# Moving the padding between SBUF tiles in a Trainium2 transformer-block kernel

## The chip, the cores and the metric

The kernel runs on one core of a Trainium2 chip. The metric is the device time of one execution, in microseconds; the median of three runs is quoted. TensorE (PE) multiplies matrices: it loads a stationary operand of 128 columns (PEld, LDWEIGHTS) and streams a moving operand of up to 512 columns past it into PSUM. VectorE (DVE) and ScalarE (ACT) do elementwise work, and DMA brings the weights from HBM into SBUF, the on-chip memory from which PE reads both operands.

## What is computed

One layer of a diffusion transformer block over 256 latent tokens and 256 context tokens, width 2048, all in float32:

```python
sh_a, sc_a, g_a, sh_m, sc_m, g_m = ada_modulation(c, w_ada, b_ada)      # 2048 x 12288
h  = modulate(rms_norm(x, norm_attn_w), sh_a, sc_a)                     # and hc for ctx
q, k, v, u = split_projection(h @ w_in)                                 # 2048 x 2560
attn = latent_window_attention(rope(q), rope(k), v, kc, vc, sink)
pool = multiscale_pool(u, pool_w, pool_scale)
x  = x + g_a * (concat([attn, pool]) @ w_out)                           # 2048 x 2048
hm = modulate(rms_norm(x, norm_mlp_w), sh_m, sc_m)
x  = x + g_m * (square(relu(hm @ w_up)) @ w_down)                       # 2048 x 8192 x 2048
return rms_norm(x, final_norm_w)
```

## The kernel before, in words

Every large product is made of three passes. Both operands are split into a high and a low part of type float32r: `hi = round(a)` on ACT (L99) and `lo = a - hi` on DVE (L100) for weights, and likewise for the activations. A product of a (stationary) and b (moving) is then `a.hi*b.hi + a.hi*b.lo + a.lo*b.hi`, all three added up in one PSUM bank. The helper `mm3` issues them as lines 290, 291 and 292, in this order.

Weights come through one stream. A load on SP's queue brings 1 MB (four slices of 128 rows by 512 columns) into one of five `raw` tiles; each half of it is split into a `hi` and a `lo` tile of 4096 bytes per partition, of which there are six each. All loads are in one fixed order, worked out beforehand, in which the loads for the modulation vectors (`ada`) lie between those of the projections.

The stages, and which operand is stationary in each:

- the input projection: for q and u (`ps_qu`) and for k (`ps_k`) the weight is stationary and the modulated tokens `hhi`, `hlo` move, 256 columns for q and u, 512 for k; for v (`ps_v`) the tokens are stationary. The first weight tile has its own order of passes, line 497;
- attention and pooling, with the pooling products `ps_pool`;
- the output projection (`ps_w`): the mixed tokens `mx` are stationary, the weights move, 512 columns;
- the first three groups of the up projection (`first_up_groups`, lines 290 to 292 with `ps_up`): the weight is stationary and the tokens `mx` move, 256 columns;
- the other thirteen up groups (`up_group`, line 920): for each quarter of the contraction first 16 products with the weight's `hi` part stationary and both parts of `mx` moving at once, 512 columns, then 16 with the `lo` part stationary and the high part of `mx` moving, 256 columns;
- the down projection (`down_group`, `ps_d`): the squared activations `ahi`, `alo` are stationary, the weights move, 512 columns. Up and down groups alternate: two up groups, then 192 down products in a row.

Tiles lie in SBUF in pools; within a pool the tags follow each other in the order in which they are first asked for, each tag with all its buffers. `gap` (L50) asks for a tile that nothing uses, and so moves what comes after it by some bytes. All tiles of the products hold a multiple of 512 bytes per partition, and so do the steps between the slices that are used as operands, so that the addresses of a tag's tiles agree modulo 512.

Lines that the change touches: L97 puts 320 bytes between the `hi` and the `lo` tiles; L448 puts 320 bytes between `hhi` and `hlo` in each of the two pools `hpa` and `hpb`; L593 puts 192 bytes ahead of the `mx` tiles in `mixa`; L598 closes `hpa` with 320 bytes; L891 puts 64 bytes between `ahi` and `alo`.

Of the kernel before, what the change touches and what calls it, by code (L numbers as in the profile page):

```python
# [9 lines left out]
F32R = mybir.dt.float32r  # L10
# [5 lines left out]
P = 128  # L16
D = 2048
KC = 16
T = 256
# [30 lines left out]
def gap(pool, n, name="gap"):  # L50

    pool.tile([P, n // 4], F32, tag=name, name=name, bufs=1)


class WeightStream:
# [28 lines left out]
    def split_to(self, n):  # L88
        nc = self.nc
        while self.n_half < min(n, len(self.halves)) and not self.hold:  # L90
            i, h = self.halves[self.n_half]
            if i >= self.n_load:
                break
            raw = self.raw[i][:, 2 * h : 2 * h + 2, :]
            hi = self.pool.tile([P, 2, 512], F32R, tag="hi", name="hi", bufs=N_HALF)
            if not self.n_half:
                gap(self.pool, 320)  # L97
            lo = self.pool.tile([P, 2, 512], F32R, tag="lo", name="lo", bufs=N_HALF)
            up = nc.scalar.copy(hi, raw)  # L99
            low = nc.vector.tensor_tensor(lo, raw, hi.bitcast(F32), ALU.subtract)  # L100
            self.last = (up.ins, low.ins)
            self.split[i, h] = (hi, lo)
            self.n_half += 1
# [23 lines left out]
def kernel(  # L127
# [223 lines left out]
    hpa = hpa_es.enter_context(tc.tile_pool(name="hpa", bufs=1, side="right", reuse_waits="tile"))  # L351
# [48 lines left out]
    def normalize(i):  # L400

        ss4 = stp.tile([P, 4], F32, tag="ss4", name="ss4", bufs=2)
        ss = stp.tile([P, 1], F32, tag="ss", name="ss", bufs=2)
        for q in range(4):
            junk = stp.tile([P, 512], F32, tag="junk", name="junk", bufs=2)
            xq = xh[i][:, 512 * q : 512 * q + 512]
            if q % 2:
                nc.scalar.activation(junk, xq, AF.Square, accum_out=ss4[:, q : q + 1])
            else:
                nc.vector.scalar_tensor_tensor(junk, xq, 1.0, xq, ALU.mult, ALU.mult, accum_out=ss4[:, q : q + 1])  # L410
        nc.vector.tensor_reduce(ss, ss4, axis=AX.X, op=ALU.add)
        r = rstd(stp, ss, 1)
        nc.vector.tensor_scalar(xh[i], xh[i], r, None, ALU.mult)
        for g in range(4):
            tp = bank("tp")
            for j in range(4):
                k = 4 * g + j
                nc.tensor.transpose(tp[:, P * j : P * j + P], xh[i][:, P * k : P * k + P], ident)
            nc.scalar.copy(xT[g][:, :, P * i : P * i + P], tp.rearrange("p (j t) -> p j t", j=4))
# [22 lines left out]
    def modulated(c_, streams=(0, 1)):  # L442

        pool = hpb if c_ in (2, 3, 6, 7) else hpa
        if 0 in streams:
            hhi = pool.tile([P, 2, 512], F32R, tag="hhi", name="hhi", bufs=2)
            if c_ in (0, 2):
                gap(pool, 320, "gaph")  # L448
            hlo = pool.tile([P, 2, 512], F32R, tag="hlo", name="hlo", bufs=2)
            hparts[c_] = hhi, hlo  # L450
        hhi, hlo = hparts[c_]
        for j in range(2):
            k = 2 * c_ + j
            xk = xT[k // 4][:, k % 4, :]
            for s in streams:
                v = xk[:, T * s : T * s + T]
                nc.vector.tensor_scalar(v, v, am_a[:, k, s : s + 1], sm_a[:, k, s : s + 1], ALU.mult, ALU.add)
            ts_ = slice(T * streams[0], T * streams[-1] + T)
            up = nc.scalar.copy(hhi[:, j, ts_], xk[:, ts_])
            low = nc.vector.tensor_tensor(hlo[:, j, ts_], xk[:, ts_], hhi[:, j, ts_].bitcast(F32), ALU.subtract)  # L460
            hs[k] = lambda s, j=j: (hhi[:, j, s], hlo[:, j, s])
        return up.ins, low.ins
# [87 lines left out]
    def run_in(op):  # L550
        if op[0] == "ada":
            c_, kg = op[1:]
            if kg == 0:
                adas[c_] = ada_attn(c_)
            adas[c_][kg]()
        elif op[0] == "mod":
            adas[op[1]][4]()
            modulated(op[1])
        elif op[0] == "kv":
            project_kv(*op[1:])  # L560
        elif op[0] == "qu":
            project_qu(*op[1:])
        elif op[0] == "mean":
            pool_mean(op[1])
        elif op[0] == "mixb":
            open_mixb()
        elif op[0] == "pool":
            in_w["pool"] = S.next("w")
        elif op[0] == "poolp":
            pool_project(op[1])  # L570
        elif op[0] == "pools":
            pool_split(op[1])
        else:
            run_late(1)

    mixa = hpb = None

    cast, sub = modulated(0, (0,))
    S.hold = False
    with tc.issue_after(sub):  # L580
# [4 lines left out]
    for op in in_ops:  # L585
        if op[0] == "ctx":
            with tc.issue_after(first_split[0]), tc.issue_after(first_split[1]):
                normalize(2)
                normalize(3)
            modulated(0, (1,))  # L590
            xn_es.close()
            mixa = ctx.enter_context(tc.tile_pool(name="mixa", bufs=1, side="left", reuse_waits="tile"))
            gap(mixa, 192)  # L593
            hpb = hpb_es.enter_context(tc.tile_pool(name="hpb", bufs=1, side="left", reuse_waits="tile"))
            gap(hpb, 192)
        else:
            run_in(op)
    gap(hpa, 320)  # L598
    st_es.close()
    hpa_es.close()  # L600

# [222 lines left out]
    mp = ctx.enter_context(tc.tile_pool(name="mp", bufs=1, side="right", reuse_waits="tile"))  # L824
# [63 lines left out]

    def activation(pss):
        ahi = mp.tile([P, 4, T], F32R, tag="ahi", name="ahi", bufs=3)  # L890
        gap(mp, 64)  # L891
        alo = mp.tile([P, 4, T], F32R, tag="alo", name="alo", bufs=3)
        for m in range(4):
            t = mp.tile([P, T], F32, tag="act", name="act", bufs=2)
            if pss[m].shape[1] == T:
                nc.scalar.activation(t, pss[m], AF.Relu)
                nc.vector.tensor_tensor(t, t, t, ALU.mult)
            else:
                nc.scalar.copy(t, pss[m][:, T : 2 * T])
                nc.vector.tensor_tensor(t, pss[m][:, 0:T], t, ALU.add)  # L900
                nc.vector.scalar_tensor_tensor(t, t, 0.0, t, ALU.max, ALU.mult)
            nc.scalar.copy(ahi[:, m, :], t)
            nc.vector.tensor_tensor(alo[:, m, :], t, ahi[:, m, :].bitcast(F32), ALU.subtract)
        return ahi, alo

    def up_group():

        pss = [bank("ps_up") for _ in range(4)]
        for kg in range(4):
            w = S.next("w")
            for part in range(2):
                for m in range(4):
                    for j in range(4):
                        k = 4 * kg + j
                        wk = w(j, slice(P * m, P * m + P))[part]
                        ps, h = (pss[m][:, 0:T], hm[k][0]) if part else (pss[m], hm[k][2])
                        nc.tensor.matmul(ps, wk, h, start=part == k == 0, stop=part == 1 and k == KC - 1, skip_group_check=True)  # L920
        return activation(pss)

    def first_up_groups():

        banks = [bank("ps_up") for _ in range(6)]
        sums = [[banks[2 * f + m // 2][:, T * (m % 2) : T * (m % 2) + T] for m in range(4)] for f in range(3)]
        acts = []  # L930
        modulate_m(0)
        for kg in range(4):
            for f in range(3):
                w = S.next("w")
                if kg == f == 0:
                    with tc.issue_after(rb_ready.ins):
                        run_late(LATE_NORM)
                for m in range(4):
                    for j in range(4):
                        k = 4 * kg + j  # L940
                        mm3(sums[f][m], w(j, slice(P * m, P * m + P)), hm[k], k == 0 and m % 2 == 0, k == KC - 1)
                with tc.issue_after(rb_ready.ins):
                    run_late(LATE_UP[3 * kg + f])
                    if kg == 2 and f == 1:
                        run_late(1)
                if kg < 3 and f == 1:
                    modulate_m(kg + 1)
                if kg == 3:
                    acts.append(activation(sums[f]))
        return acts  # L950
# [152 lines left out]
```

## Time and profile before

| what | value |
|---|---|
| median of 3 runs | 1156.07 us (1155.22 to 1157.96) |
| the profiled execution, its own time | 1154.18 us |
| its span, first to last instruction | 1152.4 us |
| mean granted TensorE clock in it | 0.99 |
| PE busy | 1109.2 us, 96% of the span |
| DVE busy | 801.9 us, 70% |
| ACT busy | 504.9 us, 44% |
| HBM read | 283.50 MB |

The profiled execution lies 1.9 us below the median of the runs. A matmul's duration in the trace is longer than the distance in time from its start to the next one's, because matmuls overlap in the array's pipeline. So a busy share of 100% on PE says only that one matmul follows another; how fast they follow is seen from starts, or from durations of the same shape that are compared with each other.

### The profile page before, as it was taken

What the parts mean: (1) busy time and instruction counts of PE and PEld (TensorE: products, weight loads), DVE (VectorE), ACT (ScalarE), POOL (GpSimd) and SP (SyncE); (2) the same over time, 40 slices, a digit from 0 to 9 for tenths busy, and PEclk for the clock granted to TensorE, in tenths of its full rate; (3) what the DMA queues carried; (4) which work ended last, traced back from release to release, by engine and by line L of the source; (5) the groups of instructions that cost most, each with busy time, mean ns of one, the idle gap of its engine ahead of it and who ended that gap; (6) DMA issues with size and microseconds to landing.
All of it is one profiled execution on the core that took longest, in us unless ns stands there. A gap on an engine that the chain in (4) does not pass through costs nothing.

```text
span 1152.4 us, 16086 instructions
## 1 busy us (share of the span) xinstructions
PE 1109.2 (96%) x6332; PEld 903.4 (78%) x6332; DVE 801.9 (70%) x1286; ACT 504.9 (44%) x762; POOL 35.5 (3%) x53
## 2 busy tenths in 40 slices
PE   4999999979999989999999999999999999999996
PEld 3767778746578869988888888888888888888885
DVE  5655557988787888796775774784664665587576
ACT  4623233377634443365433444433444443443452
POOL 1000001610000000000000000000000000000000
PEclk9999999999999989999999999999999999999998
DMA  9999897667897999977775775676556556556532
GB/s 341 358 342 345 274 332 265 212 237 272 278 380 266 311 324 343 354 257 248 272 247 184 255 268 197 239 260 205 186 189 200 192 183 184 192 188 203 183 110 74
DMA packets 174012, 286.66 MB, mean 249 GB/s; under 512 B 5608, under 2 KB 72352, under 8 KB 172784
## 3 DMA queue, kind: packets, MB, share of 16 engines
q1 hardware_dynamic: 172800, 279.55, 72.4%
q0 software_dynamic: 848, 5.55, 1.3%
q8 instruction: 50, 0.82, 0.3%
q10 hardware_dynamic: 288, 0.52, 0.1%
q14 instruction: 26, 0.21, 0.1%
HBM read 283.50 MB, written 2.10 MB: 248 GB/s over the span
## 4 chain that ended last, share of the span: by engine, by line
PE 80%; DVE 9%; DMA 6%; ACT 2%; issue 1%; SPq 0%; POOL 0%; ACTq 0%; DVEq 0%
PE ps_up L920 25%; PE ps_d L290 10%; PE ps_d L291 10%; PE ps_d L292 10%; PE ps_ada L307 5%; DMA raw<-in_w_mlp_up_dram 3%; DVE lo L100 3%; PE ps_qu L290 2%; PE ps_qu L292 2%; PE ps_qu L291 2%; DVE ada_v L329 1%; PE ps_o L764 1%; PE ps_w L290 1%; PE ps_w L292 1%; PE ps_w L291 1%
## 5 line engine op out<-in xcount | busy, mean ns | idle before, releaser
L100 DVE TENSOR_TENSOR lo<-raw,hi 128x1024 fp32r<-128x1024 f32 x330 | 396.9, 1224 | 210.4 <-ACT hi L99 203.8
L99 ACT CAST hi<-raw 128x1024 fp32r<-128x1024 f32 x330 | 337.7, 1050 | 414.5 <-PE ps_up L920 150.6
L290 PE MATMUL ps_d<-hi,ahi 128*128 128x512 f32 (+1 forms) x520 | 202.8, 391 | 0.0
L291 PE MATMUL ps_d<-lo,ahi 128*128 128x512 f32 (+1 forms) x520 | 202.3, 390 | 0.0
L920 PE MATMUL ps_up<-mx,hi 128*128 128x512 f32 x832 | 200.0, 392 | 0.0
L292 PE MATMUL ps_d<-hi,alo 128*128 128x512 f32 (+1 forms) x520 | 199.8, 388 | 0.0
L920 PEld LDWEIGHTS ps_up<-mx,hi 128*128 128x128 f32 x832 | 153.4, 188 | 31.8 <-issue 1.9
L292 PEld LDWEIGHTS ps_d<-hi,alo 128*128 128x128 f32 x520 | 97.7, 188 | 22.4
L290 PEld LDWEIGHTS ps_d<-hi,ahi 128*128 128x128 f32 x520 | 97.8, 188 | 21.7
L291 PEld LDWEIGHTS ps_d<-lo,ahi 128*128 128x128 f32 x520 | 97.7, 188 | 20.7
L329 DVE SCALAR_TENSOR_TENSOR ada_v<-raw,c_sil,ada_v 128x512 f32<-128x512 f32 x135 | 100.8, 747 | 14.7 <-DMA raw<-in_w_ada_dram 13.1
L920 PEld LDWEIGHTS ps_up<-mx,lo 128*128 128x128 f32 x832 | 105.3, 189 | 4.0
L920 PE MATMUL ps_up<-mx,lo 128*128 128x256 f32 x832 | 106.6, 281 | 0.0
L307 PE MATMUL ps_ada<-raw,c_sil 128*32 128x512 f32 x480 | 70.8, 625 | 0.9 <-DMA raw<-in_w_ada_dram 0.9
L290 PE MATMUL ps_qu<-hhi,hi 128*128 128x256 f32 x240 | 69.8, 292 | 1.4 <-ACT hi L99 1.4
L292 PE MATMUL ps_qu<-hhi,lo 128*128 128x256 f32 x240 | 67.4, 284 | 0.3 <-DVE lo L100 0.3
L291 PE MATMUL ps_qu<-hlo,hi 128*128 128x256 f32 x240 | 67.3, 281 | 0.0
L290 PEld LDWEIGHTS ps_qu<-hhi,hi 128*128 128x128 f32 x240 | 45.4, 189 | 16.6 <-issue 9.2
L290 PE MATMUL ps_up<-mx,hi 128*128 128x256 f32 x192 | 54.0, 290 | 1.6 <-ACT mx L885 1.5
L291 PE MATMUL ps_up<-mx,hi 128*128 128x256 f32 x192 | 53.5, 283 | 0.0
L292 PE MATMUL ps_up<-mx,lo 128*128 128x256 f32 x192 | 52.4, 283 | 0.0
L290 PE MATMUL ps_w<-hi,mx 128*128 128x512 f32 x128 | 51.4, 402 | 0.0
(199 smaller groups left out, 1323.1 us busy)
## 6 DMA issues: line engine op xcount, KB each, us to landing
raw<-in_w_ada_dram SPq DMA_DIRECT2D x128, 512.0 KB, 7.5
raw<-in_w_mlp_up_dram SPq DMA_DIRECT2D x64, 1024.0 KB, 5.4
raw<-in_w_mlp_down_dram SPq DMA_DIRECT2D x64, 1024.0 KB, 5.1
raw<-in_w_ada_dram SPq DMA_DIRECT2D x32, 1024.0 KB, 6.2
raw<-in_w_in_dram SPq DMA_DIRECT2D x19, 1024.0 KB, 7.6
raw<-in_w_out_dram SPq DMA_DIRECT2D x16, 1024.0 KB, 7.8
xnat<-in_x_dram SPq DMA_DIRECT2D x2, 1024.0 KB, 6.0
xnat<-in_ctx_dram SPq DMA_DIRECT2D x2, 1024.0 KB, 11.6
```

The source lines that it names most:

```text
L99: up = nc.scalar.copy(hi, raw)
L100: low = nc.vector.tensor_tensor(lo, raw, hi.bitcast(F32), ALU.subtract)
L290: nc.tensor.matmul(ps, a[0], b[0], start=first, stop=False, skip_group_check=True)
L291: nc.tensor.matmul(ps, a[0], b[1], start=False, stop=False, skip_group_check=True)
L292: nc.tensor.matmul(ps, a[1], b[0], start=False, stop=last, skip_group_check=True)
L307: nc.tensor.matmul(ps[32 * j : 32 * j + 32, :], c_sil[:, 4 * kg + j, :], raw[:, j, :], start=(kg == 0), stop=(kg == 3), tile_position=(0, ...
L329: nc.vector.scalar_tensor_tensor(box["e"], raw[:, j, :], sc, box["e"], ALU.mult, ALU.add)
L764: nc.tensor.matmul(ps[64 * i : 64 * i + 64, 0:T], va[k // 2][:, k % 2, 64 * g : 64 * g + 64], pT[:, k, i, :], start=(k == 0), stop=(k == 3 ...
L920: nc.tensor.matmul(ps, wk, h, start=part == k == 0, stop=part == 1 and k == KC - 1, skip_group_check=True)
```

## The change

All three products of a pass are left as they are; no instruction is added, removed or moved. Only places in SBUF change. The 320 bytes between `hi` and `lo` and those between `hhi` and `hlo` go, and with them the 192 bytes ahead of `mx`; the last gap of `hpa` shrinks from 320 to 128 bytes; the 64 bytes between `ahi` and `alo` move behind `alo`. The two-buffer tags `hhi` and `hlo` become two tags each with one buffer, by the chunk's parity, so that the order in the pool is `hhi0, hlo0, hhi1, hlo1`.

```diff
             hi = self.pool.tile([P, 2, 512], F32R, tag="hi", name="hi", bufs=N_HALF)
-            if not self.n_half:
-                gap(self.pool, 320)
             lo = self.pool.tile([P, 2, 512], F32R, tag="lo", name="lo", bufs=N_HALF)
...
         if 0 in streams:
-            hhi = pool.tile([P, 2, 512], F32R, tag="hhi", name="hhi", bufs=2)
-            if c_ in (0, 2):
-                gap(pool, 320, "gaph")
-            hlo = pool.tile([P, 2, 512], F32R, tag="hlo", name="hlo", bufs=2)
+            hhi = pool.tile([P, 2, 512], F32R, tag=f"hhi{c_ % 2}", name="hhi", bufs=1)
+            hlo = pool.tile([P, 2, 512], F32R, tag=f"hlo{c_ % 2}", name="hlo", bufs=1)
             hparts[c_] = hhi, hlo
...
             mixa = ctx.enter_context(tc.tile_pool(name="mixa", bufs=1, side="left", reuse_waits="tile"))
-            gap(mixa, 192)
             hpb = hpb_es.enter_context(tc.tile_pool(name="hpb", bufs=1, side="left", reuse_waits="tile"))
             gap(hpb, 192)
...
-    gap(hpa, 320)
+    gap(hpa, 128)
...
         ahi = mp.tile([P, 4, T], F32R, tag="ahi", name="ahi", bufs=3)
+        alo = mp.tile([P, 4, T], F32R, tag="alo", name="alo", bufs=3)
         gap(mp, 64)
-        alo = mp.tile([P, 4, T], F32R, tag="alo", name="alo", bufs=3)
```

## Rows read from the trace of the kernel before

**Rows 1.** The stages: busy time of each engine in stretches of the span.
```profile
core 0: us, PE busy (x) PEld busy (x) DVE busy (x) ACT busy (x) POOL busy (x), PEclk, DMA share, GB/s
26.00:209.00 183.00, 179.28 (x1307) 138.65 (x1308) 115.43 (x204) 71.42 (x102) 10.99 (x14) 0.99 0.97 322
309.00:396.00 87.00, 87.00 (x400) 69.88 (x399) 68.80 (x88) 35.67 (x48) 0.76 (x1) 1.00 0.94 325
420.00:495.00 75.00, 72.72 (x605) 71.82 (x598) 63.80 (x95) 32.33 (x43) 0.00 (x0) 0.98 0.97 334
495.00:540.00 45.00, 45.00 (x199) 36.64 (x198) 33.46 (x47) 26.27 (x41) 0.00 (x0) 1.00 0.84 284
540.00:1140.00 600.00, 600.00 (x3023) 507.40 (x3022) 393.29 (x503) 252.84 (x330) 0.53 (x1) 1.00 0.61 201
```

**Rows 2.** The chain that ended last, by line: 540 to 1140 us.
```profile
by line: PE ps_up L920 48.0%; PE ps_d L290 17.2%; PE ps_d L291 17.1%; PE ps_d L292 17.0%; PE ps_gm L965 0.6%; DVE t L1004 0.1%; DVE rs_y L277 0.0%; issue 0.0%
```

**Rows 3.** The chain's share by line, 420 to 495 us, and pieces 480 to 497 us.
```profile
by line: DMA raw<-in_w_mlp_up_dram 41.4%; DVE lo L100 17.0%; PE ps_up L290 7.0%; DVE ada_v L329 6.9%; issue 6.0%; PE ps_up L291 5.7%; ACT hi L99 5.6%; PE ps_up L292 5.6%; DVE x2T L883 1.7%; PE ps_adac L337 1.4%; DVE mx L886 0.8%; ACT mx L88
...
480.73 0.52 ACT mx L885
481.29 1.65 PE ps_up L290 x6
```

**Rows 4.** PE's groups by shape, 495 to 1140 us: count, busy us, mean ns.
```profile
L920 PE MATMUL ps_up<-mx,hi 128*128 128x512 f32 x832 | 200.0, 392 | 0.0
L290 PE MATMUL ps_d<-hi,ahi 128*128 128x512 f32 x504 | 198.4, 395 | 0.0
L291 PE MATMUL ps_d<-lo,ahi 128*128 128x512 f32 x504 | 197.8, 394 | 0.0
L292 PE MATMUL ps_d<-hi,alo 128*128 128x512 f32 x504 | 195.4, 391 | 0.0
L920 PE MATMUL ps_up<-mx,lo 128*128 128x256 f32 x832 | 106.6, 281 | 0.0
```

**Rows 5.** PE's timeline in one up group: start us, us to the last end, count.
```profile
613.71 3.81 PE L920 MATMUL ps_up<-mx,hi 128*128 128x512 f32 x16
617.37 2.05 PE L920 MATMUL ps_up<-mx,lo 128*128 128x256 f32 x16
619.25 2.46 PE L920 MATMUL ps_up<-mx,hi 128*128 128x512 f32 x10
```

**Rows 6.** The same sixteen products: the first four (613.73 to 614.5 us), later ones (615.2 to 617.2 us).
```profile
L920 PE MATMUL ps_up<-mx,hi 128*128 128x512 f32 x4 | 1.1, 394 | 0.0
...
L920 PE MATMUL ps_up<-mx,hi 128*128 128x512 f32 x11 | 2.7, 389 | 0.0
```

**Rows 7.** Down products early in a group, 563.45 to 563.75 us, mean ns.
```profile
L291 PE MATMUL ps_d<-lo,ahi 128*128 128x512 f32 x1 | 0.4, 389 | 0.0
L290 PE MATMUL ps_d<-hi,ahi 128*128 128x512 f32 x1 | 0.4, 389 | 0.0
L292 PE MATMUL ps_d<-hi,alo 128*128 128x512 f32 x1 | 0.4, 388 | 0.0
```

**Rows 8.** 256-column products: L920 `lo` (617.6 to 618.9 us), line 497 (31.1 to 31.5 us).
```profile
L920 PE MATMUL ps_up<-mx,lo 128*128 128x256 f32 x14 | 1.8, 281 | 0.0
...
L497 PE MATMUL ps_qu<-hlo,hi 128*128 128x256 f32 x6 | 0.9, 283 | 0.0
```

**Rows 9.** Products of `ps_k` and `ps_w`: duration ns min/median/max, first and last start.
```profile
L290 PE MATMUL ps_k<-hhi,hi x32: 388/396/502, 50.7 to 184.3; 128*128 128x512 f32 x32
L291 PE MATMUL ps_k<-hlo,hi x32: 389/397/502, 51.1 to 184.5; 128*128 128x512 f32 x32
...
L290 PE MATMUL ps_w<-hi,mx x128: 387/395/792, 309.3 to 405.1; 128*128 128x512 f32 x128
L291 PE MATMUL ps_w<-lo,mx x128: 387/395/398, 309.7 to 405.4; 128*128 128x512 f32 x128
L292 PE MATMUL ps_w<-hi,mx x128: 390/393/402, 309.9 to 405.6; 128*128 128x512 f32 x128
```

**Rows 10.** DVE's groups, 540 to 1140 us: the split, and one of the same size.
```profile
L100 DVE TENSOR_TENSOR lo<-raw,hi 128x1024 fp32r<-128x1024 f32 x212 | 254.2, 1222 | 176.2 <-ACT hi L99 170.0 <-PE ps_up L920 6.0
...
L993 DVE TENSOR_TENSOR y<-y,x 128x1024 f32<-128x1024 f32 x4 | 4.9, 1223 | 0.1
```

## The prediction

> **What bounds the kernel.** I looked first at the stages [rows 1]. From 26 to 495 us the sixteen DMA engines are nearly full in the three stretches that hold most large products (share 0.94 to 0.97, 322 to 334 GB/s). [...] The chain of waits says the same. From 540 to 1140 us it is 99% matmuls of the up and down groups [rows 2]; from 420 to 495 us it is DMA for 41%, DVE's splits for 17%, and products for 18% [rows 3]. So a matmul that takes less or more time counts after 495 us, and hardly before.
>
> How long does a product take there? One run of sixteen 512-column products starts at 613.71 us and the next run, of 256 columns, at 617.37: 228.8 ns each. That run ends where the following one starts, at 619.25: 117.5 ns each [rows 5]. The durations are about 162 ns longer than these spacings (281 - 117.5 = 163), so a nanosecond more in a duration is a nanosecond more of time, and I calculate with durations.
>
> The rows that matter are these: products of one shape don't take one time. In the down stage the three passes take 395, 394 and 391 ns [rows 4]; in an up group the first four 512-column products after a change of width take 394 ns, the later ones settle at 389 [rows 6]. No wait lies between them.
>
> **What the change does to the distances.** No row shows an address; I work them out from the tile sizes and the order in the pools. Let D be the start of the next product's stationary tile less that of the moving tile, modulo 512. Counting from `hi`, the kernel before has `lo` at 320, `mx` at 0, `hhi` at 192, `hlo` at 0, `ahi` at 256, `alo` at 320. After: `lo` 0, `mx` 0 (320 and 192 bytes fewer ahead of it make 512), `hhi` and `hlo` 192, `ahi` and `alo` 256. Hence:
>
> - down (`ps_d`): D is 256, 0, 256 over the three passes, and becomes 256 throughout;
> - up, L920: D stays 0 for the 512-column products, and goes from 320 to 0 for those of 256 columns;
> - first up groups: 0, 320, 0 becomes 0; output projection: 0, 192, 0 becomes 0;
> - q, u and k: 320 before and after, but their two moving tiles then lie alike; v: 192 before and after.
>
> **Part by part.** *Down, 1512 products.* A steady D has an example: the later L920 products, D = 0, settle at 389 ns [rows 6]. D = 256 has only short ones. Each of the eight down groups begins with D = 256, 0, 256, 256, 0; the third and fourth products, the two with D = 256 in a row, take 388 and 389 ns, the same settled value, and a product with D = 0 ends it [rows 7]. I take it that without this break the products stay at 389. Mean now: (395 + 394 + 391)/3 = 393.3; 393.3 - 389 = 4.3 ns, times 1512 is 6.5 us. Each of eight stretches needs some eight products at 394 to settle, 8 x 8 x 5 ns = 0.3 us. Term: **-6.2 us**. Bounds: -6.5, and above nothing: D = 320 throughout, as in k, has medians of 396 and 397 [rows 9], so 396.5 - 393.3 = 3.2 ns, +4.8 us. I take the near end because rows 7 are of this very D and these tiles.
>
> *Up, 256 columns, 832 products.* At D = 320 they take 281 ns. The first products of line 497 with `hlo` moving have D = 0, and six of them in a row, at the same width and the same tile offsets as after the change, take 283 [rows 8]. 2 ns x 832 = **+1.7 us**. Bounds: 0, if the up group settles otherwise, and +3.3 at twice that.
>
> *Up, 512 columns.* D is as before; only the state in which a run starts differs. A run takes 3.66 us, sixteen settled products would take 16 x (389 - 162) = 3.63, so some 0.03 us of unsettled start per run, 52 runs: 1.5 us that could go, or grow by as much. Taken at 0.
>
> *First up groups, 576 products.* 2 ns each would be 1.2 us, but DMA and the splits lead until about 481 us [rows 3]. From 481.29 to 495 us PE leads: 13.7 us at 117.5 ns are 117 products, **+0.2 us**. The DMA waits cover the rest; without them it is 1.2.
>
> *Output projection, 384 products.* Medians of 395, 395 and 393 [rows 9] against 389 make 5.3 ns, 2.0 us at most. The DMA engines are 94% full there [rows 1], so PE would only wait longer for weights. Taken at 0, bounds -2.0 and 0. The input projection has the same cover (0.97); q, u and k keep their D: 0, bounds 0.6 us either way (1 ns on 600 products that PE leads).
>
> *The rest.* No instruction, DMA or wait is added, and no queue is reordered. Chunks of equal parity shared a buffer before and do so after, so the tags by parity add no wait. DVE's split writes `lo` at another offset from `hi`; it takes 1222 ns, and another operation of this size over quite different tiles 1223 [rows 10], so I take no change. It is hidden behind PE, with DVE busy 393 of 600 us [rows 1]; uncovered, 1 ns on 330 splits would be 0.3 us.
>
> Sum: -6.2 + 1.7 + 0.2 = -4.3 us. The profiled execution's own time is 1154.18 (span 1152.4 plus 1.8 around it), which gives 1149.9; against the median, 1.9 us higher, it is **1151.8 us**.
>
> [...] Rows 6 show one product shape at 394 and at 389 ns with nothing waited for, so something other than the shape sets the pace. [...]
>
> **Rivals.** *(a) The distance is not the cause.* The pace of 393 in the down stage could come from the triple itself, which loads one stationary tile twice, and the 389 in rows 7 from the start of the group. Then nothing changes: 1156.1 us. Against it: the same triple shows 388 and 389 just where D repeats. Its chance takes in the case in which the down products settle halfway and the up terms take that back.
>
> *(b) A steady D = 256 settles high.* Place: the 1512 down products; mechanism: a repeated distance locks the pattern of each product onto the next, and it locks onto the pace of k (396 to 397 ns [rows 9]) instead of 389. Price: up to +4.8 us, with the up terms +6.7, 1162.8 us; at 395.5 it is +3.3 + 1.9 = +5.2, 1161.3. It decides when the down mean exceeds 393.3 + 0.3 = 393.6 ns, since 1.9 us from the up terms then make 2.3 us. For it: k has a steady D and is slow. Against it: k's moving tiles alternate between two offsets, which the down stage will no longer do.
>
> *(c) Only the up terms come* while the down stage stays: +1.9 us, 1158.0, within what counts as the same.
>
> **Chances.** A difference under 0.2%, 2.3 us, can hardly be told from none. Forecast: 0.58. (a) and (c) together: 0.23. (b): 0.19. The forecast's own range is 1148.3 (1.5 from the starts of the up runs, 2 from the output projection) to 1153.7; the whole range goes from 1148.3 up to 1160.5, which takes in (a), (c) and the lower part of (b).
>
> **What would show it.** Right: L290 to L292 of `ps_d` all at 389 to 390 ns; L920 with 256 columns at 283, with 512 columns still at 392; the stretches before 495 us as long as they were; the end of the last down product some 4 us earlier. Wrong: `ps_d` at 393 again (a), at 395 or more (b), or `ps_up` products of 256 columns still at 281; or DMA waits on PE after 495 us, which would mean that the time gained there is handed back.

## The result, and the profile after

The kernel after takes 1149.59 us (median of 13 runs, 1145.84 to 1152.87), the kernel before, measured beside it, 1156.07 us (13 runs, 1152.94 to 1160.27). The ratio is 0.9947, with a 95% interval from 0.9933 to 0.9961: 0.5% faster, more than the 0.2% that can be told from none. The forecast was 1151.8. The profiled execution took 1148.15 us, with a span of 1146.3; that is 6.0 us under the one of before.

Every engine carries out the same instructions in the same order as before; only addresses differ. Lines have moved up: 288 to 290 are now `mm3`, 915 the up groups. First PE's groups by shape over the whole span (the products of 512 columns in `ps_d`, and both shapes of L915, all start after 494 us), to be held against [rows 4].

```profile
L915 PE MATMUL ps_up<-mx,hi 128*128 128x512 f32 x832 | 200.1, 393 | 0.0
L288 PE MATMUL ps_d<-hi,ahi 128*128 128x512 f32 x504 | 195.5, 389 | 0.0
L289 PE MATMUL ps_d<-lo,ahi 128*128 128x512 f32 x504 | 195.5, 389 | 0.0
L290 PE MATMUL ps_d<-hi,alo 128*128 128x512 f32 x504 | 194.1, 389 | 0.0
L915 PE MATMUL ps_up<-mx,lo 128*128 128x256 f32 x832 | 107.9, 283 | 0.0
```

All three passes of the down products stand at 389 ns, where they were at 395, 394 and 391. Their busy time falls from 198.4 + 197.8 + 195.4 = 591.6 to 585.1 us, by 6.5. The 256-column products of the up groups take 283 instead of 281 ns and 1.3 us more in all; those of 512 columns stay within 0.1 us. The three together make -5.1 us.

The path agrees. These are the rows of `ps_d` by first pass, before and then after (duration in ns min/median/max, first and last start in us).

```profile
L290 PE MATMUL ps_d<-hi,ahi x520: 274/395/402, 495.4 to 1141.8; 128*128 128x512 f32 x168, 128*128 128x256 f32 x6
```

```profile
L288 PE MATMUL ps_d<-hi,ahi x520: 277/389/396, 494.5 to 1135.7; 128*128 128x512 f32 x168, 128*128 128x256 f32 x6
```

From the first down product to the end of the span it was 1152.4 - 495.4 = 657.0 us and is 1146.3 - 494.5 = 651.8: **-5.2 us**, where the durations say -5.1. So here what the products gained in duration came out at the end, and nothing took it back. The same stretch is my measure for the experiments, since it shuts out all that scatters before it. The stretch from 540 to 1140 us [rows 1, 2] reads as before. The window (the columns are those of rows 1) has PE busy for 596.26 us, that is without a gap until its last product ends at 1136.3:

```profile
540.00:1140.00 600.00, 596.26 (x3034) 509.53 (x3033) 397.44 (x527) 253.19 (x331) 0.53 (x1) 1.00 0.61 202
```

and the chain that ended last is made of the same products, by line:

```profile
by line: PE ps_up L915 48.1%; PE ps_d L288 16.8%; PE ps_d L289 16.8%; PE ps_d L290 16.8%; PE ps_gm L960 0.4%; DVE rs_u L280 0.2%; DVE rs_y L283 0.1%; DVE t L999 0.1%; DVE y L1005 0.1%; DVE t L1000 0.1%; DVE x L1020 0.1%; issue 0.1%; DVE rs_
```

The output projection's products (`ps_w`, as in [rows 9]) went to 389 ns too:

```profile
L288 PE MATMUL ps_w<-hi,mx x128: 387/389/799, 308.4 to 402.5; 128*128 128x512 f32 x128
L289 PE MATMUL ps_w<-lo,mx x128: 387/389/397, 308.7 to 402.7; 128*128 128x512 f32 x128
L290 PE MATMUL ps_w<-hi,mx x128: 388/389/398, 308.9 to 402.9; 128*128 128x512 f32 x128
```

but from the first of them to the first down product it is 494.5 - 308.4 = 186.1 us, as it was before (495.4 - 309.3 = 186.1). Nothing of that arrives. The remaining 0.9 us of the 6.0 lie ahead of the first `ps_w` (309.3 and 308.4).

### The profile page after: what moved, and what is told of

It is laid out like the page before. It is cut to its first block, busy times and chain, and to the rows that moved or that the text cites. A ratio compares the mean times of both kernels' runs of the same rounds, so it can differ in the third digit from the quotient of the medians.

```text
span 1146.3 us, 16086 instructions
## 1 busy us (share of the span) xinstructions
PE 1104.4 (96%) x6332; PEld 905.9 (79%) x6332; DVE 801.2 (70%) x1286; ACT 505.1 (44%) x762; POOL 35.6 (3%) x53
## 4 chain that ended last, share of the span: by engine, by line
PE 85%; DVE 8%; DMA 3%; ACT 2%; issue 1%; SPq 0%; POOL 0%; ACTq 0%; DVEq 0%
PE ps_up L915 25%; PE ps_d L288 10%; PE ps_d L289 10%; PE ps_d L290 10%; PE ps_ada L305 5%; DVE lo L98 2%; PE ps_up L288 2%; PE ps_qu L288 2%; PE ps_up L289 2%; PE ps_up L290 2%; PE ps_qu L290 2%; PE ps_qu L289 2%; PE ps_o L759 2%; DVE ada_v L327 1%; PE ps_w L288 1%
## 5 line engine op out<-in xcount | busy, mean ns | idle before, releaser
L915 PE MATMUL ps_up<-mx,hi 128*128 128x512 f32 x832 | 200.1, 393 | 0.0
L288 PE MATMUL ps_d<-hi,ahi 128*128 128x512 f32 (+1 forms) x520 | 200.0, 386 | 0.0
L289 PE MATMUL ps_d<-lo,ahi 128*128 128x512 f32 (+1 forms) x520 | 200.0, 386 | 0.0
L915 PEld LDWEIGHTS ps_up<-mx,hi 128*128 128x128 f32 x832 | 153.4, 188 | 31.8 <-issue 1.9
L915 PEld LDWEIGHTS ps_up<-mx,lo 128*128 128x128 f32 x832 | 106.7, 191 | 4.0
L915 PE MATMUL ps_up<-mx,lo 128*128 128x256 f32 x832 | 107.9, 283 | 0.0
```

What stands on the lines that cost most here:

```text
L288: nc.tensor.matmul(ps, a[0], b[0], start=first, stop=False, skip_group_check=True)
L289: nc.tensor.matmul(ps, a[0], b[1], start=False, stop=False, skip_group_check=True)
```

## The experiments

The prediction's reason is **theory 1**: a distance D from the moving to the next stationary operand that stays the same from product to product lets the products settle at 389 ns. Its rival, **theory 2**: D has no part in it; what counts is that the two moving tiles, `hi` and `lo`, lie alike. In the change both come at once. In a2, s1, t1, b1 and b2 the work tile `t` of `last_sums` comes from another pool, since there was no room for it; this changes no instruction.

### a1: only the stationary tiles apart

The kernel after, with the 64 bytes back between `ahi` and `alo`; D is 256, 320, 256.

```diff
         ahi = mp.tile([P, 4, T], F32R, tag="ahi", name="ahi", bufs=3)
-        alo = mp.tile([P, 4, T], F32R, tag="alo", name="alo", bufs=3)
         gap(mp, 64)
+        alo = mp.tile([P, 4, T], F32R, tag="alo", name="alo", bufs=3)
```

> The kernel after, with the 64 bytes between ahi and alo put back, and nothing else. In the down products the moving tiles all lie alike, and D is 256, 320, 256 over the three passes. Theory 1 (a steady distance is what lets the products settle): the down products go back to a mean of about 393 ns from 389, 1512 x 4 ns = 6 us, so about 1155.5 us. Theory 2 (it is enough that the moving tiles lie alike): they stay at 389 ns and the time at about 1149.6 us. The up products stay at 283 ns (256 columns) by both.

Measured: 1155.52 us (10 runs), ratio to before 0.9995, interval 0.9985 to 1.0005. The groups of the down products by shape, from 495 us on:

```profile
L290 PE MATMUL ps_d<-hi,alo 128*128 128x512 f32 x504 | 198.1, 397 | 0.0
L289 PE MATMUL ps_d<-lo,ahi 128*128 128x512 f32 x503 | 196.6, 392 | 0.0
L288 PE MATMUL ps_d<-hi,ahi 128*128 128x512 f32 x503 | 195.6, 390 | 0.0
```

The mean is 393 again, and the stretch from the first down product to the end is 658.3 us. Moving tiles that lie alike don't suffice here: theory 2 falls. 64 bytes ahead of one tile are worth the whole gain, 393 against 389 ns.

### a2: D = 256 throughout, both pairs apart

The kernel before, with `alo` 320 bytes behind `ahi` as `lo` is behind `hi`. So D is 256 after each pass.

```diff
-        gap(mp, 64)
+        gap(mp, 320)
         alo = mp.tile([P, 4, T], F32R, tag="alo", name="alo", bufs=3)
+        gap(mp, 256, "gap2")
```

> The kernel before, with alo moved to 320 bytes behind ahi (modulo 512), so that D is 256 in all three passes of the down products while the moving tiles hi and lo still lie 320 bytes apart; a work tile of the last stage lies in another pool to make room. Theory 1: the down products settle at 389 ns, the up products of 256 columns stay at 281 ns (D = 320), the output projection stays at 393 to 395 ns: 1156.1 - 6.5 = about 1149.6 us, and perhaps 1 to 2 us less than the kernel after from the up products. Theory 2: the down products stay at 393 ns, 1156 us.

Measured: 1156.34 us (12 runs), ratio 1.0013 (0.9999 to 1.0026), 657.0 us from the first down product.

```profile
L290 PE MATMUL ps_d<-hi,ahi 128*128 128x512 f32 x504 | 198.5, 395 | 0.0
L291 PE MATMUL ps_d<-lo,ahi 128*128 128x512 f32 x504 | 198.0, 394 | 0.0
L292 PE MATMUL ps_d<-hi,alo 128*128 128x512 f32 x504 | 195.5, 392 | 0.0
```

These are the durations of before, [rows 4], to a nanosecond. A steady D doesn't bring 389 ns here either: theory 1 falls.

### u1, u2 and u3: D swept in the up groups

The up groups are the better test bench: in each sixteen both operands come from one tag each, and D is set by where `mx` lies. The kernel after, with the `mx` tiles of the four quarters of the contraction (named `mxa` to `mxd`) 0, 64, 128 and 192 bytes further on (u1), the same and 256 more (u2), the same and 32 more (u3). The edit of u1:

```diff
-            gap(hpb, 192)
+            gap(hpb, 128)
...
+        if j in (4, 8, 12):
+            gap(pool, 64, f"gapm{j}")
+        both = pool.tile([P, 2, T], F32R, tag=f"mx{j}", name=f"mx{'abcd'[j // 4]}{j}", bufs=1)
...
```

> The kernel after, with the mx tiles of the four quarters of the contraction 0, 64, 128 and 192 bytes further on, so D of the up products is 0, 448, 384, 320 in the four quarters, and D of the output projection 0, 64, 128, 192; steady within each run of 16 or 24 products. Theory 1 in its simple form (any steady D settles alike): 512-column products end each run at 389 ns in every quarter, those of 256 columns at 281 to 283. Theory 1 with a price for each D: the settled duration differs between quarters by several ns, 396 at D = 320 as in the k products. Theory 2: as the simple form.

> As the sweep before, with 256 bytes more: D of the up products is 256, 192, 128, 64 in the four quarters, D of the output projection 256, 320, 384, 448. Simple form of theory 1: 389 ns for 512 columns in all, 281 to 283 for 256. With a price for each D: several ns between the quarters; at D = 256 it must be 389, as in the down products of the kernel after.

> The first sweep with 32 bytes more: the mx tiles of the four quarters lie 32, 96, 160 and 224 bytes further on than in the kernel after, so D of the up products is 224, 160, 96, 32 modulo 256 in the four quarters. If the pace falls off smoothly between the multiples of 64, the settled durations lie between those of the first sweep: 389 to 398 ns for 512 columns, 279.6 to 283 for 256. If the step that counts is 64 bytes, each quarter repeats one of the first sweep. A duration below 389 or 279.6 ns would be a distance that beats the kernel after.

One run each: 1150.66, 1151.44 and 1149.56 us. The groups by shape, u1:

```profile
L917 PE MATMUL ps_up<-mxa,hi 128*128 128x512 f32 x208 | 51.3, 399 | 0.0
L917 PE MATMUL ps_up<-mxd,hi 128*128 128x512 f32 x208 | 50.7, 396 | 0.0
L917 PE MATMUL ps_up<-mxb,hi 128*128 128x512 f32 x208 | 50.7, 398 | 0.0
L917 PE MATMUL ps_up<-mxc,hi 128*128 128x512 f32 x208 | 50.5, 395 | 0.0
L917 PE MATMUL ps_up<-mxa,lo 128*128 128x256 f32 x208 | 27.0, 283 | 0.0
L917 PE MATMUL ps_up<-mxc,lo 128*128 128x256 f32 x208 | 26.8, 281 | 0.0
L917 PE MATMUL ps_up<-mxb,lo 128*128 128x256 f32 x208 | 26.6, 280 | 0.0
L917 PE MATMUL ps_up<-mxd,lo 128*128 128x256 f32 x208 | 26.6, 281 | 0.0
```

u2 has the same eight numbers; two of its rows:

```profile
L918 PE MATMUL ps_up<-mxb,hi 128*128 128x512 f32 x208 | 50.7, 398 | 0.0
L918 PE MATMUL ps_up<-mxc,lo 128*128 128x256 f32 x208 | 26.8, 281 | 0.0
```

**256 bytes more change none of the eight means (399, 398, 395 and 396 ns at 512 columns, 283, 280, 281 and 281 at 256, `mxa` to `mxd`, in u1 and in u2): as far as these two runs show, the distance counts modulo 256**, not 512. With that a2 fits, at 395, 394 and 392 ns. Modulo 256 its four tiles lie as those of before do (`hi` 0, `lo` 64, `ahi` 0, `alo` 64), and the D of before, 256, 0, 256, had been steady all along.

The mean of `mxa` is no settled value: each up group begins with it, in some behind the short products for `gate_m` with a first duration of some 800 ns (799 in the profile of after), and the next ones are unsettled. In the second half of one such run, 607.65 to 609.6 us, and of the next quarter's, 613.45 to 615.25 us, u1 has:

```profile
L917 PE MATMUL ps_up<-mxa,hi 128*128 128x512 f32 x10 | 2.4, 390 | 0.0
...
L917 PE MATMUL ps_up<-mxb,hi 128*128 128x512 f32 x9 | 2.3, 397 | 0.0
```

Taken over the last eight products of each complete sixteen, the settled means in ns are:

```
D modulo 256     0     32     64     96    128    160    192    224
512 columns    389.7  395.5  395.8  396.5  394.8  394.7  397.5  395.0
256 columns    283.3  281.0  281.3  279.5  282.2  281.9  279.6  279.0
```

(0, 64, 128 and 192 from u1, the others from u3. The steps between the distances are set by the edits; that the first is 0 is worked out from tile sizes, as in the prediction, since no row shows an address.) In the table, with 512 columns, only D = 0 gives 389 (389.7); all others stand 5 to 8 ns above. With 256 columns it is the other way: D = 0 is the dearest, by up to 4 ns (283.3 against 279.0).

### s1: down tiles alike, at other distances

The kernel after, with the three buffers of `ahi` and `alo` as tags of their own (a, b, c), 64, 128 and 192 bytes further on. Within a product's triple both pairs stay alike; D is 64, 128 or 192 modulo 256.

```diff
...
+        b = "abc"[n % 3]
+        if n < 3:
+            gap(mp, 64, f"gapa{b}")
+        ahi = mp.tile([P, 4, T], F32R, tag=f"ahi{b}", name=f"ahi{b}", bufs=1)
+        alo = mp.tile([P, 4, T], F32R, tag=f"alo{b}", name=f"alo{b}", bufs=1)
+        if n == 2:
+            gap(mp, 384)
...
```

> The kernel after, with the three buffers of ahi and alo 64, 128 and 192 bytes further on than there (named a, b, c), so the down products have alike moving tiles, alike stationary tiles and a steady D of 64, 128, 192 modulo 256; a work tile of the last stage lies in another pool to make room. By the first sweep (settled durations depend on D modulo 256): about 396, 395 and 397 ns, mean 396 against 389, 1512 x 7 ns = 10.6 us slower than the kernel after, about 1160 us and so slower than the kernel before. If only alike tiles counted: 389 ns and 1149.6 us.

Measured: 1154.94 us (10 runs), ratio 0.9991 (0.998 to 1.0002), 659.4 us from the first down product. Some of its groups, from 495 us on:

```profile
L288 PE MATMUL ps_d<-hi,ahia 128*128 128x512 f32 x186 | 73.1, 395 | 0.0
L290 PE MATMUL ps_d<-hi,aloa 128*128 128x512 f32 x186 | 72.8, 395 | 0.0
L288 PE MATMUL ps_d<-hi,ahib 128*128 128x512 f32 x160 | 63.2, 395 | 0.0
L290 PE MATMUL ps_d<-hi,aloc 128*128 128x512 f32 x156 | 61.4, 395 | 0.0
L289 PE MATMUL ps_d<-lo,ahic 128*128 128x512 f32 x156 | 61.3, 393 | 0.0
L288 PE MATMUL ps_d<-hi,ahic 128*128 128x512 f32 x156 | 61.1, 391 | 0.0
```

None of the three distances reaches a mean of 389 (391 to 395): alike isn't enough here, the value counts. The size expected was too high, because in this run one distance settled in more than one way. Of buffer c, twelve durations in a row from the middle of a stretch that starts at 561.08 us, and four from one that starts at 583.28 us:

```
561.08   395 388 392 394 389 392 394 389 392 394 388 392    stretch of 39: mean 391.6
583.28   398 398 398 398                                    stretch of 24: mean 397.5
```

### t1: `lo` 192 bytes on, `alo` at three places

The kernel after with 192 bytes between `hi` and `lo`, and `alo` 0, 128 and 192 bytes off `ahi` (tags a, b, c). It asks whether moving tiles that lie apart can be had cheaply, since D = 192 makes the 256-column up products shorter.

```diff
+            if not self.n_half:
+                gap(self.pool, 192)
             lo = self.pool.tile([P, 2, 512], F32R, tag="lo", name="lo", bufs=N_HALF)
...
+            gap(mixa, 320)
...
+        if n in (1, 2):
+            gap(mp, (128, 64)[n - 1], f"gapa{b}")
+        alo = mp.tile([P, 4, T], F32R, tag=f"alo{b}", name=f"alo{b}", bufs=1)
...
```

The 320 bytes in `mixa` and the 192 make 512, so `mx` stays where it was modulo 512.

> The kernel after, with lo 192 bytes behind hi, and the three alo buffers 0, 128 and 192 bytes behind ahi (a, b, c). The up products of 256 columns have D = 192: 279.6 ns by the first sweep instead of 283, 832 x 3.4 ns = 2.8 us less. The down products have unlike moving tiles: 392 to 396 ns, 5 to 10 us more, so 1152 to 1157 us in all. If one of the three offsets of alo gives a down mean under 390.9 ns, that one would beat the kernel after.

Measured: 1157.4 us (10 runs), ratio 1.0015 (0.9997 to 1.0033), 659.1 us from the first down product. Wherever `alo` lies, the mean of a triple is above 389 ns: by the buffer of `alo` about 392 (a, where `alo` lies like `ahi`), 394 (b) and 395 (c). The up products are at 279:

```profile
L290 PE MATMUL ps_d<-hi,ahi 128*128 128x512 f32 x504 | 198.3, 395 | 0.0
L291 PE MATMUL ps_d<-lo,ahi 128*128 128x512 f32 x504 | 197.9, 394 | 0.0
L926 PE MATMUL ps_up<-mx,lo 128*128 128x256 f32 x832 | 106.5, 279 | 0.0
L292 PE MATMUL ps_d<-hi,aloa 128*128 128x512 f32 x188 | 72.7, 390 | 0.0
```

So here the moving tiles had to lie alike too. With a1 this gives both halves: the moving pair apart by itself (a) costs more than half of the 4.3 ns, the stationary pair apart by itself (a1) costs nearly all of them.

### c1: everything 64 bytes further on

All tiles of the products of the kernel after moved together; distances stay, addresses change.

```diff
+    gap(wp, 64)
     S = WeightStream(nc, wp)
...
-    gap(hpa, 128)
+    gap(hpa, 64)
...
+        gap(mp, 64)
         ahi = mp.tile([P, 4, T], F32R, tag="ahi", name="ahi", bufs=3)
         alo = mp.tile([P, 4, T], F32R, tag="alo", name="alo", bufs=3)
-        gap(mp, 64)
```

> The kernel after, with all operand tiles of the projections (hi, lo, hhi, hlo, mx, ahi, alo) 64 bytes further on, so that every distance is the same and every address another. If distances and alike tiles are the whole of it: down 389 ns, up 283 and 392 to 393 ns, 1149.6 us. If the addresses themselves count (modulo 256): the down products at another duration, 394 to 398 ns, and 1156 us or more.

Measured: 1149.71 us (5 runs), ratio 0.994 (0.9918 to 0.9961), 652.0 us from the first down product.

```profile
L289 PE MATMUL ps_d<-hi,ahi 128*128 128x512 f32 x504 | 195.5, 389 | 0.0
L290 PE MATMUL ps_d<-lo,ahi 128*128 128x512 f32 x504 | 195.5, 389 | 0.0
L291 PE MATMUL ps_d<-hi,alo 128*128 128x512 f32 x504 | 194.1, 389 | 0.0
```

Counts, times and durations in these three rows are those of after. For this shift of 64 bytes, the places themselves made no difference (389 ns in all three passes).

### h1: `hhi` and `hlo` apart again

The kernel after with that one part of the change undone, for the 1.4 us by which the input projection seemed shorter (first `ps_qu` to the first products of attention: 181.1 us before, 179.7 after).

```diff
-            hhi = pool.tile([P, 2, 512], F32R, tag=f"hhi{c_ % 2}", name="hhi", bufs=1)
-            hlo = pool.tile([P, 2, 512], F32R, tag=f"hlo{c_ % 2}", name="hlo", bufs=1)
+            hhi = pool.tile([P, 2, 512], F32R, tag="hhi", name="hhi", bufs=2)
+            if c_ in (0, 2):
+                gap(pool, 320, "gaph")
+            hlo = pool.tile([P, 2, 512], F32R, tag="hlo", name="hlo", bufs=2)
...
-    gap(hpa, 128)
+    gap(hpa, 320)
```

> The kernel after, with hhi and hlo 320 bytes apart as in the kernel before. If alike tiles are what shortened the input projection (from its first product to the first attention score 181.1 us before, 179.7 after; 179.9 to 180.1 in the sweeps, which have them alike), it takes 181.2 us here, and everything behind it is 1.2 us later until DMA evens it out; the rival, that this is scatter, gives any value between 179.7 and 181.3. Down products 389 ns by both.

One run: 1150.28 us, 651.8 us from the first down product, and 181.4 us for the stage. That looks like the answer, but c1 and b1, in which the two tiles lie alike, have 181.0 and 181.3. The stage scatters by as much as was to be explained: inconclusive. The products themselves are 1 to 2 ns shorter with the tiles alike. The largest group, q and u by the first pass, after and then in h1:

```profile
L288 PE MATMUL ps_qu<-hhi,hi 128*128 128x256 f32 x240 | 69.3, 290 | 1.4 <-ACT hi L97 1.4
```

```profile
L288 PE MATMUL ps_qu<-hhi,hi 128*128 128x256 f32 x240 | 69.8, 292 | 1.4 <-ACT hi L97 1.4
```

Over the three passes it is 203.3 against 204.5 us of busy time, 1.2 us at most, in a stage with a DMA share of 0.97 (26 to 209 us, in before [rows 1] and in after).

### b1 and b2: both widths at their best distance

The table asks for D = 0 in the down stage and D = 224 (b1) or 192 (b2) for the 256-column up products. The `lo` tiles become 256 bytes longer, and only the weights of the up projection put their low part 224 or 192 bytes further on in them.

```diff
...
-            lo = self.pool.tile([P, 2, 512], F32R, tag="lo", name="lo", bufs=N_HALF)
+            lo = self.pool.tile([P, 1088], F32R, tag="lo", name="lo", bufs=N_HALF)
+            at = 56 if i in self.moved else 0
+            lo = lo[:, at : at + 1024].rearrange("p (j c) -> p j c", j=2)
...
     def add_up(f, kg):
+        S.moved.add(len(S.items))
...
```

> The kernel after, with lo tiles 256 bytes longer; weights of the up projection put their lo part 224 bytes further on in the tile, all others at its start. The up products of 256 columns then have D = 224 modulo 256: 279 ns by the third sweep instead of 283, 832 x 4 ns = 3.3 us less. The lo tiles of the down projection lie alternately at 0 and 256 modulo 512: if 256 bytes is the period, the down products stay at 389 ns and the time is about 1149.6 - 3.3 = 1146.3 us, ratio to before 0.991 to 0.993. If the period is 512, the down products go to 393 ns and the time to about 1152 us.

> As the one before with 192 bytes: D = 192, 279.6 ns by the first sweep, 2.8 us less than the kernel after, 1146.8 us. Whether the change back from 256 to 512 columns costs more or less than before decides between the two by some tenths of a us.

Measured: b1 1147.77 us (6 runs), ratio to before 0.9928 (0.9907 to 0.995); b2 1147.76 us (4 runs), 0.9932 (0.9914 to 0.9949). b1's groups, then two of b2's:

```profile
L918 PE MATMUL ps_up<-mx,hi 128*128 128x512 f32 x832 | 200.4, 393 | 0.0
L291 PE MATMUL ps_d<-hi,ahi 128*128 128x512 f32 x504 | 195.5, 389 | 0.0
L918 PE MATMUL ps_up<-mx,lo 128*128 128x256 f32 x832 | 105.5, 279 | 0.0
```

```profile
L918 PE MATMUL ps_up<-mx,hi 128*128 128x512 f32 x832 | 201.6, 394 | 0.0
...
L918 PE MATMUL ps_up<-mx,lo 128*128 128x256 f32 x832 | 106.5, 279 | 0.0
```

Against after, b1's `lo` products give 2.4 us and its `hi` products take 0.3: -2.1. From the first down product to the end it is 649.9 us, 1.9 less than after. In b2 the two sums, -1.4 and +1.5, cancel, and the stretch is 652.1. There a run of 512 columns behind 256-column products takes ten products to come to 389 ns, where b1 and after take five. The `lo` tiles in both lie 0 or 256 modulo 512 in turn, and the down products stay at 389: 256 bytes make no difference here either. (Both have the work tile `t` in the other pool, so that move by itself costs the down products nothing.) Both kernels beat the one before. That they beat the one after isn't shown by the times, since the intervals of the ratios overlap; the profile shows it for b1's last stretch, in one execution.

## Why the prediction was right, and where its reason was wrong

**The down products: size right, reason wrong.** The term was -6.2 us with 389 ns for all three passes; it measured 389 and -6.5. But I had it from "D = 256, 0, 256" becoming "256 throughout", and read [rows 7] as a steady distance broken by a product with D = 0. The same rows spoke against it: their second product, with D = 0 by that count, stands at 389 too. Modulo 256 these two values are one, and in a2 a steady D gained nothing with the tiles of each pair apart (395, 394 and 392 ns). The step that failed is the sentence "I take it that without this break the products stay at 389": the break was no change of D but the low tiles, 64 bytes off in the moving and in the stationary operand. That the size came out right all the same was luck: the change also put both pairs alike, on which the term did not rest. In place of the steady distance the runs give three conditions, of which the change meets all:

```
kernel   offsets modulo 256: hi  lo  ahi  alo      ps_d, ns by pass      first ps_d to end, us
before                       0   64   0   64       395 / 394 / 391       657.0
a2                           0   64   0   64       395 / 394 / 392       657.0
a1                           0    0   0   64       390 / 392 / 397       658.3
t1                           0  192   0   0,128,192   395 / 394 / 390-394   659.1
s1                           0    0  64,128,192 (both)   391-395          659.4
after                        0    0   0    0       389 / 389 / 389       651.8
```

The moving tiles lie alike, the stationary tiles lie alike, and the distance between the two is 0 modulo 256: of these kernels only after has all three, and only after has 389 ns in all three passes. Which pair of tiles a product feels is only in part settled. The moving tile and the next stationary one can't be all of it: in before and a2 their distance is 0 modulo 256 after every pass, and the mean is 393. Nor can one moving tile and the next: they lie alike in a1 and s1, which are slow. A product's own two tiles would be enough for this table by themselves, since a distance of 0 between them in all three passes is the three conditions in other words; but then it is odd that the first pass of before, whose own distance is 0, is its slowest. No run takes that apart.

**Up groups.** At 256 columns +1.7 us was forecast at 283 ns; it is 283 ns and +1.3 us. The value came from the six products of [rows 8], which by the table had D = 0 modulo 256, as after; the 281 of before had D = 64. At 512 columns 0 was forecast and 0.1 came.

**What DMA covers.** For the output projection I said that products at 389 would only wait longer, and for the first up groups +0.2 us. The two stages together take 186.1 us before and after, although the products of the first went to 389. Other kernels have 183.9 to 188.6 for the same stretch, so a microsecond there can't be read. The input projection was taken at 0 with bounds of 0.6; whether its tiles bring up to 1.2 us stays open.

**The sum.** Forecast for the part behind the first down product: -6.2 + 1.7 = -4.5; measured -5.2. Of the 0.7 between them 0.4 lie in the up term and 0.3 in the down term. The loss for settling is there, 0.2 us where 0.3 was forecast: after, each of the eight down groups begins with 396, 397 or 398, 389, 395, 393 and then 389 ns, some 25 ns too many. The rest of the difference between the forecast, -4.3, and the medians, -6.5, lies ahead of that, where this pair of profiles has -0.9, and in the scatter of the medians (the interval of the ratio allows -4.5 to -7.7 us).

**The rivals.** (a), the distance is not the cause, falls with a1: 64 bytes ahead of one tile bring 393 ns back. (c) falls with the first table. (b), a steady distance that settles high, is what happened at every other distance that was run: s1 has 391 to 395 ns, and the sweep 395 to 398. The change escaped it because its 256 gave what 0 gives in the sweep, 389 ns. I gave (b) 0.19 from the k products [rows 9], without a reason that could have told the two apart; what I held against it, that k's moving tiles alternate, was none. After the change they lie alike, D is 64 modulo 256 as before, and the medians stay high:

```profile
L288 PE MATMUL ps_k<-hhi,hi x32: 392/396/501, 50.8 to 183.1; 128*128 128x512 f32 x32
L289 PE MATMUL ps_k<-hlo,hi x32: 388/394/497, 51.1 to 183.3; 128*128 128x512 f32 x32
L290 PE MATMUL ps_k<-hhi,lo x32: 390/397/398, 51.3 to 183.6; 128*128 128x512 f32 x32
```

The nearest row for that stood beside them: the settled up products, 389 at D = 0 [rows 6]; that 256 bytes more leave the means as they are (u1 and u2) I didn't know.

**One tile, two paces.** a1 and after issue the same products in the same order with one tile 64 bytes off, and the third pass takes 397 or 389 ns, with 0.0 us of idle time of PE before it in both. So in this kernel a distance does change the pace; by what mechanism, and where in the chip, no run shows.

## What to carry to other kernels

Where PE runs without a gap, compare the durations of equal products by pass: a few nanoseconds between them, with no wait, are worth a look at the SBUF addresses of both operands. For these float32r products of 512 columns, as far as this kernel shows, place all moving tiles alike and all stationary tiles alike, at distance 0 modulo 256 bytes (389 ns in `ps_d` after; 390 to 397 by pass in a1, 391 to 395 in s1); at 256 columns in a row try 192 and 224 instead (279 ns in b2 and b1, 283 after). And when a change meets several conditions at once, vary each by itself before the reason is believed: the sum of a forecast can come out right with the wrong one.

## What I had not expected of the hardware

256 bytes more in the distance changed nothing (u1 and u2 have equal mean durations in all eight groups), and in the sweep the best distance at 512 columns, D = 0 with 389.7 ns, is the worst at 256, with 283.3. Nor did a distance have a single duration: in s1 the same tiles at D = 192 settle at 398, or go round in 388, 392, 394, by what came before: all five long stretches of buffer c behind one of buffer a with a mean of 394 ns take 398, and all three behind one with 395 or 396 take 392. And what ran ahead still shows behind a change of operands. Of `mxa` in u1, one sixteen behind 256-column products with D = 64, and one behind down products with D = 0 (starts in us, durations in ns):

```
807.13   394 397 398 388 393 398 389 395 393 389 390 389 389 390 389 389
873.14   389 390 390 390 389 389 389 390 389 389 389 390 390 389 389 390
```

The first needs nine products until 389 holds, which costs some 44 ns; the second goes on at 389 from its first product. Both have the same distances throughout; what differs is what ran ahead of them.
